# A two-layer decoder on one core: small matmuls of the mixer issued in whole groups, the last four gated heads kept in rows, keys' halves copied by DMA, and a reordered attention

## The chip, the core and the metric

The kernel runs on one core of a Trainium2 chip as a single program. The metric is device time in microseconds (us). The names of the engines in the profile are PE (TensorE, matmuls and transposes), PEld (its weight loads), DVE (VectorE), ACT (ScalarE), POOL (GpSimd) and SP (SyncE, whose queue issues nearly all DMAs).

## The reference

A decoder trunk for 512 tokens of width 1024. Layer 0 mixes tokens with a gated DeltaNet (8 query/key heads, 16 value heads of width 128), layer 1 with sliding-window attention over keys and values projected once (16 query heads, 4 key/value heads of width 64, window 128). Each layer ends with a gated MLP (inner width 2816) with a causal convolution.

```
def gated_deltanet(hn, w_in, conv_w, a_log, dt_bias, out_norm_w, w_out):
    proj = hn @ w_in
    qkv, z, b, a = split(proj)
    qkv = silu(causal_dwconv(qkv, conv_w))
    ...                                   # q, k, v; l2norm of q and k; beta, g
    o = chunked_gated_delta_rule(q, k, v, g, beta)
    o = rmsnorm(o, out_norm_w) * silu(z)
    return o @ w_out

def chunked_gated_delta_rule(q, k, v, g, beta):
    ...                                   # decay, m
    t_mat = triangular_solve(m + eye, eye)
    ...
    def step(state, inp):
        w_i, u_i, qd_i, kd_i, a_i, gl_i = inp
        v_new = u_i - w_i @ state
        o_i = qd_i @ state + a_i @ v_new
        state = state * gl_i + kd_i.T @ v_new
        return state, o_i

def sliding_window_sink_attention(hn, k, v, w_q, sinks, w_o, bias, mask):
    q = (hn @ w_q) * 64 ** -0.5
    s = where(mask, q @ band(k).T + bias, -1e30)
    m = maximum(max(s), sink)
    p = exp(s - m)
    o = (p / (sum(p) + exp(sink - m))) @ band(v)
    return o @ w_o
```

All of it is in float32.

## The kernel before

Activations lie transposed, 128 channels by 512 tokens to a tile. A large product is split in high and low parts: `cast` makes `whi` on ScalarE (line 132) and `wlo` on VectorE (133) from a loaded weight tile `stage`, and `mm3` issues three 128x512 matmuls for each slice of the contraction, hi·hi, hi·lo and lo·hi (lines 162 to 164, and 1181 to 1185 in attention, where they are yielded one by one). These are called dense products here. PSUM has eight banks under four names: `d` (three, dense products), `g` (two, transposes and small products), `s` (two), `p` (one).

**Mixer.** The 16 value heads go in four groups of four. The table `ORDER` is a list of jobs for each group: projections, key and query products, the triangular solve in 32x32 and then 64x64 tiles (`levels`, lines 570 to 597), four chunks of the scan (`scan`, 617 to 662), projections of the gates (z) and gates (g). A job's place in the table and `SHIFT` set the priority of its instructions; a scheduler then lays out each engine's queue by priority and by what is ready in its own cost model. So a job's instructions can be taken apart, and dense products of the next projection stand between them. `ORDER` and `SHIFT` are the same in both kernels.

In a chunk of the scan, TensorE makes `kS` and `qS` from the state `S` (line 617), `pu` from the solved tile (632), and after ScalarE has copied `pu` into `us` (636), `pS`, the product for the new state (640), and `po`, the output (657). The output goes to the scratch `od` in memory.

A gate (`gate`, 693 to 705) loads a head's output from `od` and its gate from `zd`, ScalarE scales the four quarters one by one (700), TensorE transposes each into bank `g` (703), VectorE multiplies (704), and the result is stored to `yd`. Heads 12 to 15 are gated last, behind the scan of the fourth group; they use the rows `dt` (four) and `va` (two). Then the output product `a_w_out` loads every head from `yd` (801) into rows `u`, splits it in hi and lo, loads and transposes x (821, copied at 822 by ScalarE) and adds the product to it.

**Attention.** Keys and values are projected (`attention`, 1140 on). The keys of each of the four heads are needed on both halves of the 128 partitions, since two query heads are multiplied at a time; ScalarE and VectorE write hi and lo of each half into both halves (1163 to 1167), with 64 partitions an instruction. Values are transposed at line 1171. From then on TensorE's order is written out by hand: for each of 16 steps `scores(u)` (1224), softmax on VectorE and ScalarE (1232 to 1253), `values(u - 2)` (1276), `turn_back(u - 1)`, which transposes the probabilities (1260), and 11 or 12 dense products of the next query projection or the first output tiles, by `take(stream, n)`. At the end come `values(14)`, `turn_back(15)`, `late_outputs` (1311), which ends three output tiles that were opened early, with `values(15)` before its last slice.

Between and behind these the MLPs are dense products nearly alone.

Of the kernel before, what the change touches and what calls it, by code (L numbers as in the profile page):

```python
# [41 lines left out]
def kernel(  # L42
# [137 lines left out]

    xs = []
# [25 lines left out]
    def columns(parts, n, s, q=SP, tag="acc"):  # L207
# [6 lines left out]
        ps = bank("g")  # L214
# [191 lines left out]
    def key_norms(g):  # L406
        pr = slice(2 * g, 2 * g + 2)
        st[g]["kk"] = pair("m32")
        for i in range(2):
            kT = st[g]["k"][:, i, :]  # L410
            ps = bank("g")
            for c in range(NC):
                cs = slice(c * P, (c + 1) * P)
                PE.matmul(ps[:, cs], kT[:, cs], kT[:, cs], start=True, stop=True)
# [59 lines left out]
    def query_norms(g):  # L474
        for i in range(2):
            ps = bank("g")
            junk = row("va")
            for c in range(NC):
                cs = slice(c * P, (c + 1) * P)
                PE.transpose(ps[:, cs], st[g]["q"][:, i, cs], ident[:])  # L480
                S.activation(junk[:, cs], ps[:, cs], AF.Square, accum_out=sse[:, 1, 2 * g + i, c : c + 1])
# [3 lines left out]
    def query_products(g, i):  # L485
        pq = bank("g")
        for c in range(NC):
            cs = slice(c * P, (c + 1) * P)
            PE.matmul(pq[:, cs], st[g]["k"][:, i, cs], st[g]["q"][:, i, cs], start=True, stop=True)
# [5 lines left out]
    def key_tokens(g, i):  # L495
        ps = bank("g")
        for c in range(NC):
            cs = slice(c * P, (c + 1) * P)
            PE.transpose(ps[:, cs], st[g]["k"][:, i, cs], ident[:])
# [10 lines left out]
    def value_proj(g, hh):  # L510
# [6 lines left out]
        for c in range(NC):  # L517
            cs = slice(c * P, (c + 1) * P)
            PE.transpose(ps[:, cs], v[:, cs], ident[:])
# [87 lines left out]
    def scan(g, c):  # L607
# [3 lines left out]
        hj = [(h, slice(h * P, (h + 1) * P)) for h in range(4)]  # L611
        if c > 0:
            kS, qS = bank("s"), bank("s")
            for x, t in ((kS, w["k"]), (qS, w["q"])):
                for i in range(2):
                    si = slice(256 * i, 256 * i + 256)
                    PE.matmul(x[:, si], t[:, i, cs], S0[:, si], start=True, stop=True)  # L617
            rr, qe = row("rq"), row("rq")
            for h, js in hj:
                V.scalar_tensor_tensor(  # L620
# [6 lines left out]
                )  # L627
            for h, js in hj:
                S.activation(qe[:, js], qS[:, js], AF.Copy, scale=egc[:, 4 * g + h, c : c + 1])
        pu = bank("s")  # L630
        for h, js in hj:
            PE.matmul(
                pu[:, js], w["y", h][:, cs], rr[:, js] if c > 0 else w["v", h][:, cs], start=True, stop=True
            )
        us = row("us")
        S.copy(us[:], pu[:])
        if c < NC - 1:
            pS = bank("p")
            for h, js in hj:
                PE.matmul(pS[:, js], w["kt", h][:, cs], us[:, js], start=True, stop=True)  # L640
            sn = row("S")
            if c == 0:
                V.tensor_copy(sn[:], pS[:])
            else:
                for h, js in hj:
                    V.scalar_tensor_tensor(
# [8 lines left out]
        po = bank("s")  # L655
        for h, js in hj:
# [752 lines left out]
```

## Time and profile before

| | |
|---|---|
| median of 3 runs | 1426.94 us (1426.77 to 1426.95) |
| profiled execution, its own time | 1428.72 us |
| span of the profiled execution | 1426.9 us |
| granted TensorE clock, mean | 0.998 |
| busy: PE, DVE, ACT | 1389.5, 1113.8, 753.8 us |
| mixer's heads, up to the end of the last scan | about 44 to 434 us |
| last gates, x, start of the output product | about 434 to 468 us |
| keys, values, attention | about 890 to 1028 us |

The span is from the first to the last instruction. In rows of a timeline stand the start, the length, the engine, the line, the operation with output<-inputs, the number of instructions that follow one another alike, and in brackets the idle time ahead and what ended it. A matmul in float32 has two records, so four products read x8; a transpose has one. Matmuls are pipelined: a row's length reaches from a matmul's start to its modelled end, and the next one starts earlier.

### The profile page before, as it was taken

The page shows a single profiled execution, that of the slowest core. Times are in us where ns is not written, and L with a number is a line of the kernel's source. Part 1 is how long each engine was busy: PE and PEld are TensorE (multiplying, and loading weights), DVE is VectorE, ACT ScalarE, POOL GpSimd, SP SyncE. Part 2 cuts the span into 40 slices and gives each one's busy share as a digit, 9 for nine tenths or more (in the row PEclk, how much of TensorE's full clock was granted, in tenths as well). Part 3 has the DMA queues.
Part 4 walks back from the last instruction along what each step waited for, and adds up shares of the span by engine and source line. Part 5 has one row for each costly group of instructions (what it writes and reads, how often), then busy time and mean ns, then how long its engine had stood idle before and what let it go on. Part 6 is the DMA issues. An engine that isn't in the chain of part 4 may idle for free.

```text
span 1426.9 us, 21762 instructions
## 1 busy us (share of the span) xinstructions
PE 1389.5 (97%) x8362; PEld 1165.5 (82%) x8362; DVE 1113.8 (78%) x2078; ACT 753.8 (53%) x1475; POOL 13.0 (1%) x37
## 2 busy tenths in 40 slices
PE   7999999999998999999999999999999999999997
PEld 5777878878876888888988889778788888988897
DVE  4996887969854447889878889878568888878996
ACT  7764566666546434444334446667544544344443
POOL 1000000000000000000000000000000000000000
PEclk9999999999999999999999999999999999999999
DMA  5324254264466324221443223122132322332222
GB/s 159 103 63 142 79 175 122 73 187 127 141 204 213 118 64 140 90 89 45 133 148 117 75 77 110 55 93 75 38 122 78 111 81 68 125 112 88 96 75 74
DMA packets 163131, 152.85 MB, mean 107 GB/s; under 512 B 24212, under 2 KB 150741, under 8 KB 163029
## 3 DMA queue, kind: packets, MB, share of 16 engines
q1 hardware_dynamic: 160770, 151.27, 33.0%
q8 instruction: 66, 1.08, 0.3%
q10 hardware_dynamic: 2259, 0.20, 0.1%
q14 instruction: 36, 0.29, 0.1%
HBM read 134.65 MB, written 16.80 MB: 106 GB/s over the span
## 4 chain that ended last, share of the span: by engine, by line
PE 82%; DVE 8%; DMA 6%; ACT 2%; issue 1%; DVEq 0%; SPq 0%; ACTq 0%
PE d L162 19%; PE d L163 19%; PE d L164 19%; DVE wlo L133 2%; PE s L617 1%; PE d L1030 1%; PE d L1185 1%; PE d L1028 1%; PE d L1183 1%; PE d L1181 1%; PE d L1029 1%; PE g L1260 1%; PE s L1030 1%; PE p L1276 1%; PE s L657 1%
## 5 line engine op out<-in xcount | busy, mean ns | idle before, releaser
L162 PE MATMUL d<-xh,whi 128*128 128x512 f32 x1128 | 445.1, 396 | 0.2
L163 PE MATMUL d<-xl,whi 128*128 128x512 f32 x1128 | 444.0, 395 | 0.0
L164 PE MATMUL d<-xh,wlo 128*128 128x512 f32 x1128 | 443.2, 395 | 0.7 <-DVE wlo L133 0.4
L132 ACT CAST whi<-stage 128x1024 fp32r<-128x1024 f32 (+2 forms) x234 | 227.3, 975 | 229.2 <-PE d L163 146.8
L133 DVE TENSOR_TENSOR wlo<-stage,whi 128x1024 fp32r<-128x1024 f32 (+2 forms) x234 | 263.5, 1129 | 66.7 <-ACT whi L132 66.2
L164 PEld LDWEIGHTS d<-xh,wlo 128*128 128x128 f32 x1128 | 211.6, 188 | 45.6 <-DVE wlo L133 1.1
L162 PEld LDWEIGHTS d<-xh,whi 128*128 128x128 f32 x1128 | 211.7, 188 | 44.1 <-ACT xh L172 0.5
L163 PEld LDWEIGHTS d<-xl,whi 128*128 128x128 f32 x1128 | 211.7, 188 | 42.9 <-issue 0.5
L260 DVE SCALAR_TENSOR_TENSOR acc<-d,cwc,acc 128x511 f32<-128x511 f32 (+2 forms) x96 | 70.7, 738 | 12.2 <-ACT acc L257 11.6
L911 ACT ACTIVATE dt<-dt 128x512 f32<-128x512 f32 x44 | 27.8, 632 | 80.1 <-DVE dt L894 80.1
L889 DVE TENSOR_TENSOR sz<-d,p6s 128x512 f32<-128x512 f32 x58 | 40.0, 689 | 36.9 <-PE d L164 35.0
L894 DVE SCALAR_TENSOR_TENSOR va<-sz,fcw,va 128x511 f32<-128x511 f32 (+1 forms) x58 | 43.4, 748 | 1.7 <-ACT va L892 0.9
L894 DVE SCALAR_TENSOR_TENSOR dt<-sz,fcw,dt 128x511 f32<-128x511 f32 (+1 forms) x58 | 43.4, 748 | 0.9
L546 DVE TENSOR_TENSOR sT<-sT,p6s 64x31 f32<-64x31 f32 (+15 forms) x124 | 40.8, 329 | 2.2 <-DVE p6s L540 0.3
L540 DVE TENSOR_TENSOR p6s<-sN,sT 64x31 f32<-64x31 f32 (+15 forms) x124 | 40.5, 327 | 2.4 <-DMA sN<-nd 0.4
L1249 ACT ACTIVATE dt<-dt,sm 128x256 f32<-128x256 f32 (+1 forms) x64 | 30.1, 471 | 19.2 <-DVE sm L1232 19.1
L132 ACT CAST whi<-st 128x768 fp32r<-128x768 f32 (+1 forms) x30 | 23.7, 792 | 30.1 <-PE p L1029 5.8
L889 DVE TENSOR_TENSOR zl<-d,p6s 128x512 f32<-128x512 f32 x30 | 20.7, 689 | 24.0 <-PE d L164 23.7
L665 ACT ACTIVATE rq<-o 128x128 f32<-128x128 f32 x64 | 19.0, 298 | 28.6 <-DVE o L660 16.0
L913 DVE TENSOR_TENSOR va<-dt,va 128x512 f32<-128x512 f32 x44 | 30.4, 691 | 1.2
L133 DVE TENSOR_TENSOR wlo<-st,whi 128x768 fp32r<-128x768 f32 (+1 forms) x30 | 26.9, 903 | 2.2 <-ACT whi L132 2.2
L892 ACT ACTIVATE dt<-sz,normc,fcw 128x512 f32<-128x512 f32 x29 | 23.6, 814 | 7.2 <-DVE sz L889 7.2
(770 smaller groups left out, 2866.7 us busy)
## 6 DMA issues: line engine op xcount, KB each, us to landing
stage<-in_ffn_w_up_dram SPq DMA_DIRECT2D x44, 1024.0 KB, 4.9
stage<-in_a_w_in_dram SPq DMA_DIRECT2D x23, 1024.0 KB, 5.1
stage<-in_ffn_w_down_dram SPq DMA_DIRECT2D x16, 768.0 KB, 6.1
stage<-in_a_w_out_dram SPq DMA_DIRECT2D x8, 1024.0 KB, 4.9
st<-in_ffn_w_down_dram SPq DMA_DIRECT2D x8, 768.0 KB
zd<-sz SPq DMA_DIRECT2D x16, 256.0 KB, 2.0
od<-o SPq DMA_DIRECT2D x16, 256.0 KB, 3.7
stage<-in_b_w_q_dram SPq DMA_DIRECT2D x4, 1024.0 KB
```

The lines of the kernel that those rows point to most:

```text
L132: S.copy(hi[:, :kt, :m], src)
L133: V.tensor_tensor(lo[:, :kt, :m], src, hi[:, :kt, :m].bitcast(F32), op=ALU.subtract)
L162: PE.matmul(ps, hi[:, k, :m], xh[k], start=first and k == 0, stop=False)
L163: PE.matmul(ps, hi[:, k, :m], xl[k][:], start=False, stop=False)
L164: done.append(PE.matmul(ps, lo[:, k, :m], xh[k], start=False, stop=last and k == kt - 1))
L260: V.scalar_tensor_tensor(acc[:, d:], ps[:, : T - d], col, acc[:, d:], op0=ALU.mult, op1=ALU.add)
L540: V.tensor_tensor(tv, N[:, s, s + 1 : 32].unsqueeze(2).to_broadcast([64, n, m]), Tm[:, s : s + 1, 0:m].to_broadcast([64, n, m]), op=ALU.mult,)
L546: V.tensor_tensor(Tm[:, s + 1 : 32, 0:m], Tm[:, s + 1 : 32, 0:m], tv, op=ALU.subtract)
L889: V.tensor_tensor(u[:], ps[:], rs[:], op=ALU.mult)
L894: V.scalar_tensor_tensor(acc[:, d:], u[:, : T - d], tap(2 - d, t), acc[:, d:], op0=ALU.mult, op1=ALU.add)
L913: V.tensor_tensor(b[:], a[:], b[:], op=ALU.mult)
L1249: S.activation(ej, ej, AF.Exp, bias=ngm[:, i : i + 1], scale=-1.0, accum_out=den[:, i : i + 1])
```

## The change

It has five parts.

1. A function `together` issues a group of small matmuls: the first with the order of issue behind the instructions given (the last that makes an input), the others behind the first, with a priority raised by `JUMP`, so that the scheduler lays the group out whole. `turn_row` does that for the four transposes of a row. They are used in key and query products, transposes of the mixer, the gates, the transposes of x, and the scan. The function `levels` is not edited.
2. In the scan `qS` is in bank `p`, `kS` and `qS` are one group behind the last piece of the state, `pu` is a group behind the last piece of `rr`, and `pS` and `po` are one group of eight.
3. The four last heads are gated in the rows `va`, `va`, `us` and `p6s`, and stay there for the output product; they are no longer stored to `yd` and loaded again.
4. A key pair's hi and lo are split once over 128 partitions, and four DMAs write the swapped halves. An Exp of one column goes ahead of the attention, and the values' transposes stand behind the fourth issue of `one_by_one`.
5. In the hand-written order, eight dense products go ahead of the first `turn_back` and four behind; at the end the outputs are split in other portions, and the last slice goes over the three tiles by kind of product instead of tile by tile.

```diff
+    def together(makes, *after):
+        first = None
+        for make in makes:
+            if first is None:
+                first = make()
+                for a in after:
+                    behind(first, a)
+            else:
+                with tc.high_priority(JUMP):
+                    behind(make(), first)
+
+    JUMP = 4000000
+
+    def turn_row(ps, src, *after):
+        cut = [slice(c * P, (c + 1) * P) for c in range(NC)]
+        together([lambda cs=cs: PE.transpose(ps[:, cs], src[:, cs], ident[:]) for cs in cut], *after)
...
     def scan(g, c):
-            kS, qS = bank("s"), bank("s")
+            kS, qS = bank("s"), bank("p")
+            terms = []
             for x, t in ((kS, w["k"]), (qS, w["q"])):
                 for i in range(2):
                     si = slice(256 * i, 256 * i + 256)
-                    PE.matmul(x[:, si], t[:, i, cs], S0[:, si], start=True, stop=True)
+                    terms.append((x[:, si], t[:, i, cs], S0[:, si]))
+            together([lambda a=a: PE.matmul(*a, start=True, stop=True) for a in terms], w["last"])
...
+        together([lambda a=a: PE.matmul(*a, start=True, stop=True) for a in terms], *last)
         us = row("us")
         S.copy(us[:], pu[:])
...
+            terms += [(pS[:, js], w["kt", h][:, cs], us[:, js]) for h, js in hj]
+        terms += [(po[:, js], w["at", h][:, cs], us[:, js]) for h, js in hj]
+        together([lambda a=a: PE.matmul(*a, start=True, stop=True) for a in terms])
...
     def gate(h):
-        ot, y = (row("ol"), row("zl")) if h < 12 else (row("dt"), row("va"))
+        ot = row("ol" if h < 12 else "dt")
+        y = row("zl") if h < 12 else row(("va", "va", "us", "p6s")[h - 12])
...
-            S.activation(ot[:, cs], ot[:, cs], AF.Copy, scale=f_c[:, h, c : c + 1])
+            scaled = S.activation(ot[:, cs], ot[:, cs], AF.Copy, scale=f_c[:, h, c : c + 1])
         pt = bank("g")
-        for c in range(NC):
-            PE.transpose(pt[:, c * P : (c + 1) * P], ot[:, c * P : (c + 1) * P], ident[:])
+        turn_row(pt, ot, scaled)
         V.scalar_tensor_tensor(y[:], pt[:], onw_c[:, 8:9], y[:], op0=ALU.mult, op1=ALU.mult)
-        SP.dma_start(yd[h], y[:])
+        if h < 12:
+            SP.dma_start(yd[h], y[:])
+        else:
+            gated[h] = y
...
-            yr = r2("u")
-            SP.dma_start(yr[:], yd[2 * h2 + j])
+            if h2 < 6:
+                yr = r2("u")
+                SP.dma_start(yr[:], yd[2 * h2 + j])
+            else:
+                yr = gated[2 * h2 + j]
             split(yr[:], a[:, j, :], b[:, j, :])
...
-                        S.copy(hi, src)
-                        S.copy(keys[g][far, 0, :], src)
-                        V.tensor_tensor(keys[g][near, 1, :], src, hi.bitcast(F32), op=ALU.subtract)
-                        V.tensor_tensor(keys[g][far, 1, :], src, hi.bitcast(F32), op=ALU.subtract)
+                    near, far = keys[i]
+                    split(f[:], near[:, 0, :], near[:, 1, :])
+                    for a, b in ((slice(0, 64), slice(64, 128)), (slice(64, 128), slice(0, 64))):
+                        SP.dma_start(far[a, :, :].bitcast(F32), near[b, :, :].bitcast(F32))
...
+        S.activation(warm[:], rs[:, 0:1], AF.Exp, scale=0.0)
...
+        for t in turned_values:
+            behind(t, issued[3])
...
                 if u > 1:
                     values(u - 2)
+                if u == 1:
+                    take(stream, 8)
                 if u > 0:
                     turn_back(u - 1)
-                take(stream, 12 if u < 12 else 11)
-            values(14)
+                take(stream, 4 if u == 1 else 12 if u < 12 else 11)
             for _ in stream:
                 pass
+            rest = late_outputs(opened, range(begun, KD - 1))
+            take(rest, 9)
             turn_back(15)
-            for k in range(begun, KD - 1):
-                for _ in late_outputs(opened, k):
-                    pass
+            values(14)
+            take(rest, 5)
             values(15)
-            for _ in late_outputs(opened, KD - 1):
+            for _ in rest:
                 pass
+            for i in range(3):
+                for m, (ps, w) in enumerate(opened):
+                    PE.matmul(ps[:], w[i % 2][:, KD - 1, :], (ah, ah, al)[i][-1], start=False, stop=i == 2)
+                    if i == 2:
+                        V.tensor_tensor(hT[m], hT[m], ps[:], op=ALU.add)
```

Three places of TensorE's queue show the change in order. First the solve of the fourth group, just ahead of its scan: `d` is the bank of a projection, `p` and `s` hold 64x64 tiles of the solve, `g` the transposes of a gate of an earlier group. Before:

```order
L164 MATMUL d_4405<-xh_142,wlo_4407 128x512
L703 MATMUL g_4126<-ident_81,ol_4118 128x128
L590 MATMUL p_4050<-Xg,nt_3418 64x64 x2
L703 MATMUL g_4126<-ident_81,ol_4118 128x128
L590 MATMUL p_4050<-Xg,nt_3418 64x64 x4
L703 MATMUL g_4126<-ident_81,ol_4118 128x128
L590 MATMUL p_4050<-Xg,nt_3418 64x64 x2
L703 MATMUL g_4126<-ident_81,ol_4118 128x128
L162 MATMUL d_4405<-xh_151,whi_4406 128x512
```

and the same products now, which have the lines 605 and 612:

```order
L164 MATMUL d_4404<-xh_160,wlo_4406 128x512
L605 MATMUL p_4050<-Xg,nt_3418 64x64 x8
L162 MATMUL d_4404<-xh_169,whi_4405 128x512
L163 MATMUL d_4404<-xl_170,whi_4405 128x512
L164 MATMUL d_4404<-xh_169,wlo_4406 128x512
L612 MATMUL s_4061<-sy_4001,p6s_347 64x64 x8
```

The eight small products stood in three pieces with transposes between, and are now one piece between dense products.

Second, the gates of heads 12 to 15 on TensorE, behind the last scan; `dt` is a scaled head, `d` the output product over the heads gated earlier. Before:

```order
L164 MATMUL d_4637<-sy_4522,wlo_4667 128x512
L703 MATMUL g_4332<-ident_81,dt_4324 128x128
L162 MATMUL d_4695<-kT_4512,whi_4696 128x512
L703 MATMUL g_4332<-ident_81,dt_4324 128x128 x2
L163 MATMUL d_4695<-qT_4513,whi_4696 128x512
L703 MATMUL g_4332<-ident_81,dt_4324 128x128
L164 MATMUL d_4695<-kT_4512,wlo_4697 128x512
L703 MATMUL g_4445<-ident_81,dt_4437 128x128
```

and now:

```order
L163 MATMUL d_4683<-qT_4509,whi_4684 128x512
L198 MATMUL g_4332<-ident_81,dt_4324 128x128 x4
L163 MATMUL d_4625<-at_4529,whi_4654 128x512
L164 MATMUL d_4625<-at_4528,wlo_4655 128x512
L164 MATMUL d_4683<-kT_4508,wlo_4685 128x512
L198 MATMUL g_4444<-ident_81,dt_4436 128x128 x4
```

The four transposes of a head are a whole group, with three dense products to the next head's, where they alternated with single dense products.

Third, the first `turn_back` in attention; `s` holds scores, `g` the transposed probabilities of step 0, `d` a query projection. Before:

```order
L1224 MATMUL s_8787<-kT_8384,S_8691 128x256
L1224 MATMUL s_8788<-kT_8384,S_8691 128x256
L1260 MATMUL g_8820<-ident_81,dt_8736 128x128 x2
L1260 MATMUL g_8825<-ident_81,dt_8743 128x128 x4
L1181 MATMUL d_8770<-xh_8639,whi_8771 128x512
```

and now, with eight dense products of which the first and the last two are shown in their place:

```order
L1251 MATMUL s_8768<-kT_8372,S_8672 128x256
L1251 MATMUL s_8769<-qT_8373,S_8672 128x256
L1207 MATMUL d_8751<-xh_8619,whi_8752 128x512
...
L1207 MATMUL d_8751<-xh_8627,whi_8752 128x512
L1209 MATMUL d_8751<-xl_8628,whi_8752 128x512
L1287 MATMUL g_8809<-ident_81,dt_8717 128x128 x2
L1287 MATMUL g_8814<-ident_81,dt_8724 128x128 x4
```

The transposes, which need the softmax of step 0, came right behind the scores of step 1, and now come behind eight dense products as well.

More of the change, by code (lines that the diff above doesn't have):

```diff
@@ L654, in scan @@
             w["S"] = sn
-        po = bank("s")
-        for h, js in hj:
-            PE.matmul(po[:, js], w["at", h][:, cs], us[:, js], start=True, stop=True)
         ot = row("o")
@@ L819 @@
         pt = bank("g")
-        for c in range(NC):
-            PE.transpose(pt[:, c * P : (c + 1) * P], x3[:, c, :], ident[:])
+        turn_row(pt, xrows[m])
         S.copy(hT[m], pt[:])
@@ L1141, in attention @@
         toep = rb[:]
[L1143 removed]
+        keys = [[wide("G") for u in range(2)] for i in range(2)]
         kxh, kxl = normed(h, NKV)
+        turned_values = []
         for kv in range(2):
```

70 lines of the change are left out of this document (31 added, 39 removed).

## The prediction

> **What bounds the kernel now.** I read the page first, then busy time by stretches, then TensorE's waits and the timeline around each. The page's first part says that TensorE is the bound:
>
> ```profile
> PE 1389.5 (97%) x8362; PEld 1165.5 (82%) x8362; DVE 1113.8 (78%) x2078; ACT 753.8 (53%) x1475; POOL 13.0 (1%) x37
> ```
>
> So only TensorE's own work and the 37 us in which it idles can be saved. The stretches that the change touches are the mixer up to its last chunks, the mixer's tail with the gated heads, the start of attention and its end. The columns are the window, its length, then busy time and count of each engine, granted clock, DMA.
>
> ```profile
> 44.00:420.00 376.00, 373.02 (x2685) 302.69 (x2686) 301.91 (x651) 231.93 (x594) 7.03 (x20) 1.00 0.42 128
> 420.00:470.00 50.00, 44.25 (x223) 34.23 (x222) 25.47 (x49) 30.51 (x82) 0.00 (x0) 0.97 0.62 200
> 900.00:945.00 45.00, 41.87 (x220) 32.11 (x219) 35.77 (x78) 30.41 (x62) 0.00 (x0) 1.00 0.25 81
> 1010.00:1035.00 25.00, 23.34 (x144) 17.76 (x143) 13.66 (x32) 12.20 (x26) 0.00 (x0) 1.00 0.19 62
> ```
>
> TensorE idles 3.0 us in the 376 of the mixer, where most of the grouping is done, but 5.8 in the tail, 3.1 at the start of attention and 1.7 at its end. The waits that carry this (us in total, times, longest):
>
> ```profile
> PE g L821 <- DVE va L704: 3.5, 1, 3.5
> ...
> PE g L1260 <- DVE dt L1253: 2.2, 1, 2.2
> ...
> PE g L703 <- ACT ol L700: 0.7, 2, 0.4
> ```
>
> A row of idle time understates a loss by some 0.16 us, since a dense matmul's row lasts 0.40 and the next starts after 0.24 (169.13 to 169.37 in the next lines).
>
> **Grouping 128-wide products.** Columns: start, us, engine, line, what, count. First a group of four transposes between dense products, then transposes that alternate with dense ones:
>
> ```profile
> 168.45 0.60 PE L499 MATMUL g<-ident,kT 128*128 128x128 f32 x4
> 168.81 0.49 PE L164 MATMUL d<-xh,wlo 128*128 128x512 f32 x1
> 169.13 0.40 PE L162 MATMUL d<-xh,whi 128*128 128x512 f32 x1
> 169.37 0.40 PE L163 MATMUL d<-xl,whi 128*128 128x512 f32 x1
> ```
>
> ```profile
> 444.28 0.27 PE L703 MATMUL g<-ident,dt 128*128 128x128 f32 x1
> ...
> 444.62 0.27 PE L703 MATMUL g<-ident,dt 128*128 128x128 f32 x1
> ```
>
> The group takes 169.13 - 168.45 - 0.24 = 0.44 us, 0.11 each. Singly, one dense and one transpose take 444.62 - 444.28 = 0.34, again about 0.1. So a split group costs nothing by itself, and holding these groups whole gains 0. What the hold can do is move waits: they come at the group's first member.
>
> **The solve's small tiles** are not grouped by the change, but transposes no longer stand between them. They do pay for each break:
>
> ```profile
> 399.51 0.40 PE L164 MATMUL d<-xh,wlo 128*128 128x512 f32 x1
> 399.83 0.68 PE L590 MATMUL p<-Xg,nt 64*64 64x64 f32 x16
> ...
> 400.78 0.39 PE L163 MATMUL d<-xl,whi 128*128 128x512 f32 x1
> ...
> 405.75 0.40 PE L164 MATMUL d<-xh,wlo 128*128 128x512 f32 x1
> ...
> 408.02 0.40 PE L163 MATMUL d<-xl,whi 128*128 128x512 f32 x1
> ```
>
> Whole, L590's 16 records and two dense products take 1.27 us. The same 16 in three pieces, with four transposes among them, take 2.27; less 4 x 0.11 that is 1.83, so 0.28 for each extra piece. Counted in the order, runs of small tiles go from 9, 9, 10, 14 in the four groups of heads to 9, 9, 9, 8. Seven fewer by 0.28 is **-2.0 us** (between 0, if each comes to stand alone in a wait anyway, and -3).
>
> **The tail.** First the last scan product and the first late gate, then ScalarE's scalings and one of the eight copies of x, then DMAs, then one window:
>
> ```profile
> 433.75 1.16 PE L657 MATMUL s<-us,at 128*128 128x128 f32 x8 [0.34 <-ACT us L636]
> ...
> 442.94 0.33 PE L703 MATMUL g<-ident,dt 128*128 128x128 f32 x1 [0.49 <-ACT dt L700]
> ```
>
> ```profile
> 442.49 4.79 ACT L700 ACTIVATE dt<-dt,fc 128x128 f32<-128x128 f32 x16 [0.57 <-DMA dt<-od]
> ...
> 460.12 0.59 ACT L822 COPY h<-g 128x512 f32<-128x512 f32 x1 [0.50 <-PE g L821]
> ```
>
> ```profile
> 438.76 3.65 DMA dt<-od
> ...
> 445.02 8.38 DMA yd<-va
> 453.42 2.53 DMA va<-zd
> ```
>
> ```profile
> 458.00:468.00 10.00, 9.91 (x50) 7.58 (x50) 2.83 (x5) 5.85 (x11) 0.00 (x0) 0.85 0.47 156
> ```
>
> Heads 14 and 15 wait for the two rows `va`, which are free only when heads 12 and 13 have been stored to `yd` (8.38 us); then 2.53 more bring `zd`. The transposes of x stand behind them in bank g, and the wait of L821 on L704 above is theirs: 3.5 + 0.16 = 3.7 us lost. Behind it the granted clock is 0.85 for 10 us: 1.5 us of clock lost. With the 0.49 + 0.16 at the first gate that makes 5.9. The Trainium skill ("TensorE: Matmul & The Clock Gate", section "Why this matters for your kernels") warns of TensorE gaps above some 3 us, after which the clock falls to half. This trace agrees that a gap of 3.5 is followed by a lower clock, though by 0.85 in the mean over 10 us. By that rule the 1.5 goes with the gap, as I count it; were a gap above 3 us left, the tail would gain 1.5 less.
>
> Now each of the four heads has a row of its own, so `zd` is loaded long before, and four stores and four loads of `yd` leave SP's queue. Two of the early loads, into `us` and `p6s`, wait there until these rows are free; the one into `us` stands ahead of the last `od` store, but waits for the products that this store's data need too, so I cost it at 0. What is late next is `dt<-od` and ScalarE: the 16 scalings take 4.79, 1.2 a head, and the first head's group now waits for all four of its quarters, until 442.49 + 1.2 = 443.7. TensorE was through with its dense products 0.49 + 0.16 before 442.94, at 442.3; counted in the order, 34 of them now stand between the last product of the scan (the eight of 433.75) and the first gate, for 32 before, so it comes at 442.8 and loses 0.9 + 0.16 = 1.1 us. The later heads come 1.2 apart with three dense products and a group, 3 x 0.24 + 0.44 = 1.2, between them. Then eight copies of x and four casts of the same size, 12 x 0.59 = 7.1 us of ScalarE, stand against TensorE's 11 dense products and 32 transposes, 6.2: 0.9 more. So 5.9 - 2.0 = **-3.9 us**; the ends are -5.9 and -2.0, if a wait of some 3 us stays.
>
> **Scans and gates of the other heads.** Each scan loses and gains waits: in the last one the products of `S` now have dense ones ahead, but one chunk's pu is followed at once by pS and po, which need `us`, copied by ScalarE (a copy as large as that at 460.12, 0.59). I take 0, between -2.7 (nearly all of the mixer's 3.0 of idling) and +4.
>
> **Attention's start.** Before, the keys' halves were cut and copied by 8 + 8 instructions of half height:
>
> ```profile
> 910.90 0.68 DVE L1166 TENSOR_TENSOR kT<-va,kT 64x512 fp32r<-64x512 f32 x1
> ...
> 923.04 1.23 DVE L133 TENSOR_TENSOR wlo<-stage,whi 128x1024 fp32r<-128x1024 f32 x1
> ```
>
> ```profile
> 917.28 1.25 PE L1171 MATMUL g<-ident,va 128*128 128x128 f32 x8 [0.63 <-DVE va L1158]
> ```
>
> Two of full height on each engine replace them: VectorE loses six of 0.70, 4.2 us, and the values that L1171 waits for are ready earlier; these transposes also move nine dense products back. Its wait and the slow starts around it go: **-1.2 us** (0 to -1.3). The four key DMAs of 256 KB are new. The nearest row is `dt<-od`, 256 KB in 3.65 us; from VectorE's split at about 912 they have until 929 to land, so 0. Behind them in SP's queue is the third load of query weights, which cannot start before 923.04 + 1.23 in the trace (its buffer) and so loses nothing. The early Exp on ScalarE moves a table load into time freed by six casts: 0.
>
> Then the softmax pipeline fills:
>
> ```profile
> 929.55 0.44 PE L1224 MATMUL s<-kT,rq 64*128 64x128 f32 x4
> ...
> 942.46 1.09 PE L1260 MATMUL g<-ident,dt 128*128 128x128 f32 x8
> ```
>
> ```profile
> 932.34 0.35 DVE L1232 CUSTOM_DVE_ANT_0 dt<-s,sz,nsink 128x128 f32<-128x128 f32 x1
> ...
> 1007.06 0.35 DVE L1232 CUSTOM_DVE_ANT_0 dt<-s,sz,nsink 128x128 f32<-128x128 f32 x1 [0.32 <-PE s L1224]
> ...
> 1009.86 1.01 DVE L1253 TENSOR_SCALAR dt<-dt,sm 128x128 f32<-128x128 f32 x4
> 1012.32 0.48 DVE L1232 CUSTOM_DVE_ANT_0 dt<-s,sz,nsink 128x256 f32<-128x256 f32 x1 [1.45 <-PE s L1224]
> ...
> 1015.46 1.14 DVE L1253 TENSOR_SCALAR dt<-dt,sm 128x256 f32<-128x256 f32 x4
> ```
>
> From the first scores to the second turn-back TensorE takes 12.9 us, of which some 2.8 are waits (3.1 of idling in the stretch, less the 0.63 above, and 0.16 behind each of two) and 10.1 work. The same work is done in the new order, but eight of the twelve dense products stand ahead of the first turn-back. What ends it then is two softmaxes in a row: 2.8 until VectorE starts (932.34 - 929.55), 3.8 for an even one (1007.06 to 1010.87), 4.3 for an odd one, 10.9. So **-2.0 us** (0 to -2.8).
>
> **Attention's end.**
>
> ```profile
> 1017.35 0.44 PE L1276 MATMUL p<-acc,Vp 128*64 128x128 f32 x4 [0.70 <-DVE at L169]
> ...
> 1025.36 0.50 PE L1181 MATMUL d<-at,whi 128*128 128x512 f32 x1 [0.69 <-ACT at L168]
> ```
>
> ```profile
> 1026.62 2.94 ACT L132 CAST whi<-stage 128x1024 fp32r<-128x1024 f32 x3 [1.31 <-PE d L1183]
> ```
>
> The move of the values behind the turn-back, and four dense products behind the last values, cover both waits and a smaller one: -2.2. But all three opened weight tiles are now read until the last three products, so the next casts (0.98 each) and VectorE's low part start some six products later: I estimate +1.4 by laying those rows behind the seventh of the nine. **-0.8 us** (-2.2 to +1.9).
>
> **Sum.** -2.0 - 3.9 + 0 - 1.2 - 2.0 - 0.8 = -9.9. The profiled execution took 1428.7 with a span of 1426.9, so it would take 1418.8; the median of the runs, 1426.94, lies 1.8 below it, so the runs would show 1417.0.
>
> **Rivals.**
> (1) The grouped mixer gives part back: whole groups leave fewer dense products in a scan's waits. For: the chunk where pS follows pu at once. Against: 3.0 us of idling in 376. Price +5 (the upper end above, and a wait as long as that at 433.75 in three more scans), so 1422.0.
> (2) The change doesn't do what it says in the tail and the fill: ScalarE's copies and `od` take `zd`'s place and VectorE's chain sets the fill as before. Then the tail keeps its wait of some 3 us (1.9 of the gain missing) and the fill's 2.0 are gone: 1420.9. For: ScalarE is busy 30.5 of 50 us there.
> (3) Slower: holding a gate's group until the fourth quarter is scaled costs up to three quarters of 0.30 us, 0.9, at each of 16 gates, 14.4 us. It outdoes the gain from 0.62 a gate on; in full, 1431.4. Against: only 0.7 us in two waits at L703 for the first twelve, and the order puts more dense products ahead.
>
> **How the numbers follow.** The forecast has 0.60, rivals 1 and 2 0.17 each, rival 3 0.06. A measurement here can tell about 0.2%, 2.9 us. The forecast's own bounds of scans, tail and end reach some 6 us below and 4 above; with rivals 1 and 2 the range is 1410.5 to 1423.5. Faster by over 0.2% (below 1424.1): the forecast and most of rivals 1 and 2, 0.88. Within 0.2%: what is left of these, 0.07. Slower: rival 3 past its point, 0.05.
>
> **What would show it.** Right: L704's successor waits for no DMA and the clock is 1.00 from 420 to 470; a single wait of 1 to 1.5 us at the first late gate; 35 runs of small tiles; under 1.2 us of waiting between the first scores and the second turn-back; a wait for whi of some 1 us after the last values. Wrong: TensorE's idling in 44 to 420 above 6 us, a gap over 3 us anywhere in the tail, or first scores that wait for a key DMA.

## The result, and the profile after

The changed kernel took 1416.98 us, median of 4 runs (1416.23 to 1418.66), beside 1426.95 for the kernel before on the same chip: a ratio of 0.9925, 95% interval 0.9909 to 0.994. The profiled execution took 1418.66 with a span of 1416.8, for 1428.72 and 1426.9 before, so 10.1 us are to be found in the two traces.

The page's busy times of the changed kernel:

```profile
PE 1384.8 (98%) x8362; PEld 1166.5 (82%) x8362; DVE 1109.1 (78%) x2072; ACT 748.0 (53%) x1470; POOL 15.7 (1%) x37
```

TensorE has the same 8362 records and is now idle for 32.0 us, not 37.4. So only 5.3 of the 10.1 us are idle time that the trace shows. Of the rest, 1.7 is the half clock that the tail no longer has, and some 3 are records of the mixer that start sooner after one another. The four stretches shown of before, the last two moved with the stage:

```profile
44.00:420.00 376.00, 371.15 (x2690) 303.91 (x2689) 304.91 (x656) 232.14 (x596) 9.66 (x20) 1.00 0.42 130
420.00:470.00 50.00, 47.70 (x247) 38.45 (x247) 28.10 (x51) 32.33 (x83) 0.00 (x0) 1.00 0.54 173
893.00:938.00 45.00, 44.85 (x253) 35.44 (x253) 33.52 (x77) 28.87 (x62) 0.00 (x0) 1.00 0.38 117
1002.00:1027.00 25.00, 23.88 (x147) 18.33 (x146) 14.41 (x30) 13.11 (x27) 0.00 (x0) 1.00 0.25 85
```

The tail went from 223 to 247 matmul records in 50 us and its clock from 0.97 to 1.00; the start of attention idles 0.15 us for 3.1. The mixer idles more than before, 4.9 us for 3.0. What TensorE waits for between 280 and 470 us, and at the end of attention:

```profile
PE d L162 <- ACT kT L168: 2.0, 1, 2.0
PE g L198 <- ACT ol L720: 1.5, 1, 1.5
PE p L659 <- ACT us L653: 1.5, 1, 1.5
PE g L198 <- ACT dt L720: 0.3, 1, 0.3
```

```profile
PE d L162 <- ACT whi L132: 1.1, 3, 0.7
```

L162 on kT waits for a load of `yd`, L198 on `ol` for a gate's load of `od`, L659 for `us` in the chunk where `pS` follows `pu` at once. The waits for rows `va` and for the softmax are gone.

Stage by stage, from the start of one row to the start of another in the two traces, with the nominal time of products that the change moved over a stage's border taken out:

| stage | before to after, us |
|---|---|
| start of the program, up to the last transpose of the input | +0.7 |
| mixer, up to the last scan product | -1.1 |
| tail and output product, up to the MLP's norm | -5.8 |
| up to the first scores (values, queries) | -1.2 |
| first scores to second turn-back | -2.4 |
| from there to the end | -0.1 |

They add up to -9.9. The start is not touched by the change: in the fourteen profiles here its last transpose begins between 16.1 and 18.0 us, whatever the kernel. The tail's borders are the last scan product and the matmul of the norm, here of the changed kernel, then of the one before (its scan product is the row at 433.75 above):

```profile
434.17 1.16 PE L659 MATMUL s<-us,at 128*128 128x128 f32 x8
...
528.79 0.69 PE L869 MATMUL g<-ones,ol 128*128 128x1 f32 x5
```

```profile
535.08 0.69 PE L845 MATMUL g<-ones,ol 128*128 128x1 f32 x5
```

That is 94.6 us for 101.3, of which 0.9 is dense work that now stands ahead of the scan product.

### The profile page after: what moved, and what is told of

It is laid out like the page before. It is cut to its first block, busy times and chain, and to the rows that moved or that the text cites. A ratio compares the mean times of both kernels' runs of the same rounds, so it can differ in the third digit from the quotient of the medians.

```text
span 1416.8 us, 21740 instructions
## 1 busy us (share of the span) xinstructions
PE 1384.8 (98%) x8362; PEld 1166.5 (82%) x8362; DVE 1109.1 (78%) x2072; ACT 748.0 (53%) x1470; POOL 15.7 (1%) x37
## 4 chain that ended last, share of the span: by engine, by line
PE 85%; DVE 7%; DMA 4%; ACT 2%; issue 1%; SPq 0%; DVEq 0%; ACTq 0%
PE d L162 20%; PE d L164 20%; PE d L163 20%; PE g L198 2%; DVE wlo L133 2%; PE d L1207 1%; PE d L1211 1%; PE d L1209 1%; PE d L1054 1%; PE d L1052 1%; PE d L1053 1%; PE s L1054 1%; PE p L1303 1%; PE s L659 1%; PE s L1052 1%
## 5 line engine op out<-in xcount | busy, mean ns | idle before, releaser
L162 PE MATMUL d<-xh,whi 128*128 128x512 f32 x1128 | 444.2, 394 | 0.2
L162 PEld LDWEIGHTS d<-xh,whi 128*128 128x128 f32 x1128 | 211.7, 188 | 44.8 <-ACT xh L172 0.5
```

Source lines behind the costliest of these rows:

```text
L162: PE.matmul(ps, hi[:, k, :m], xh[k], start=first and k == 0, stop=False)
```

## The experiments

All times are against the kernel before on the same chip in the same rounds; a ratio's interval is 95%, and 0.001 is 1.4 us. Most parts are worth 1 to 4 us, beside a scatter of single executions that is as large (31 of the kernel before, in the rounds of the first four runs, lay between 1424.1 and 1431.3). So the ratios carry the totals, and the traces the stages, each from a single execution.

**The late gates' part alone.** Parts 1, 2, 4 and 5 of the change are left out:

```diff
+        y = row("zl") if h < 12 else row(("va", "va", "us", "p6s")[h - 12])
...
+            gated[h] = y
```

> The kernel before with nothing changed but the last four gated heads: rows va, va, us and p6s, kept there, no yd store and load for them. Nothing is held in groups, the scan and the attention are as before. Theory A (the tail is most of the gain, 5.8 of 10.0 us, and needs no grouping): 1421.2 us, the wait of L821 on L704 (3.5 us) gone, no granted clock below 0.95 between 420 and 470, a wait at the first late gate of 0.3 to 0.7. Rival B (the tail gains only because its transposes come in whole groups): 1425 to 1427, a wait of over 2 us stays.

Measured: 0.9976 (0.9968 to 0.9985), -3.4 us. The tail stage fell by 5.5 us, the wait of L821 is gone with no group held, and the window has a full clock:

```profile
420.00:470.00 50.00, 47.68 (x252) 37.87 (x251) 30.63 (x54) 34.22 (x87) 0.00 (x0) 1.00 0.56 179
```

So theory A's stage holds, and the total is less than 5.8. In the profile some 3.3 us were lost elsewhere, at places that this edit does not touch. From 45.35 us the granted clock was 0.50 for 3.41 us, behind a wait of 1.75 us; all fourteen profiles have that wait near 44 us, at 1.62 to 1.93. And behind the 2.2 us wait of the first turn-back it was 0.50 again. In the run with only the groups held (below) the same wait was followed by 1.00. First rows of this run, then of that one:

```profile
PE g L1289 <- DVE dt L1282: 2.2, 1, 2.2
...
929.40:932.81 3.41, 1.20 (x12) 0.86 (x8) 2.79 (x14) 3.03 (x13) 0.00 (x0) 1.00 0.00 0
932.81:936.23 3.42, 3.42 (x11) 2.65 (x10) 1.70 (x9) 1.18 (x4) 0.00 (x0) 0.50 0.31 81
```

```profile
PE g L1275 <- DVE dt L1268: 2.2, 1, 2.2
...
930.74:934.16 3.42, 1.77 (x10) 1.52 (x11) 2.51 (x13) 2.85 (x12) 0.00 (x0) 1.00 0.02 5
934.16:937.57 3.41, 3.41 (x31) 2.63 (x32) 2.58 (x8) 2.01 (x5) 0.00 (x0) 1.00 0.28 77
```

**Own rows, with the round trip kept.** As the last, but every head is stored to `yd` and loaded again:

```diff
+        y = row("zl") if h < 12 else row(("va", "va", "us", "p6s")[h - 12])
...
         SP.dma_start(yd[h], y[:])
```

> As the kernel before, and the last four gated heads have the rows va, va, us and p6s, but each is still stored to yd and loaded again. Theory A1 (the 3.5 us wait is for the rows that the stores of heads 12 and 13 hold; own rows are enough): the wait of L821 on L704 goes, the loads of yd then feed the last products late, a wait of under 2 us for a cast of sy, at or vt: 1421 to 1423. Rival A2 (the round trip itself, 8.4 us of yd<-va and a load behind it, is what ends last): the wait moves to the products of heads 12 to 15 at 3 us or more and the clock falls again: 1425 to 1427.

Measured: 0.9988 (0.9979 to 0.9997), -1.7 us; the tail stage fell by 2.4. The wait for `va` is gone, and two waits for heads that come back from memory have taken its place:

```profile
PE d L162 <- ACT kT L168: 1.6, 1, 1.6
PE d L162 <- ACT ktok L168: 1.3, 1, 1.3
```

The waits and the full clock in the tail are theory A1's, but the total, some 1425.2 us, lies where rival A2 had it. In these profiles own rows give 2.4 of the stage and leaving out the round trip the other 3.1. This split is not firm: in the run with the eight dense products (below), whose tail is as before, the stage was 2.0 shorter as well.

**The groups alone.** Parts 1 and 2, with rows, `yd` and attention as before:

```diff
+            together([lambda a=a: PE.matmul(*a, start=True, stop=True) for a in terms], w["last"])
...
+        turn_row(pt, ot, scaled)
```

> The kernel before with only the groups of small matmuls held whole, in the whole mixer, the gates and the transposes of x, and the scan's banks and order of pS and po; rows of the late gates, yd and the attention as before. Theory A (fewer pieces of the solve, -2 to -3, against three waits in the mixer of 1.5 to 2.0 us each): 1426.0, within 1.5 of before, with waits of 1 us or more at a gate, at a pS and behind a load of yd. Rival C (the groups themselves bring the gain of the mixer and the tail): 1423 or less.

Measured: 0.9981 (0.9971 to 0.9991), -2.7 us, more than theory A had and less than rival C. The mixer stage fell by 1.2 in the trace, as in the changed kernel, with two of the three waits that I expected (1.5 at a `pS`, 1.1 at a gate, but 0.5 behind a load of `yd`). But the tail fell by 3.5 too, and I had given that stage to the rows alone:

```profile
PE g L198 <- DVE va L720: 0.7, 1, 0.7
```

That whole groups did this is not shown. VectorE's product for the first late gate starts 0.14 us sooner than before (444.10 for 444.24). The one for the third gate, which waits until a row `va` has been stored and loaded again, starts 3.2 sooner. First before, then this run:

```profile
456.07 0.75 DVE L704 SCALAR_TENSOR_TENSOR va<-g,onwc,va 128x512 f32<-128x512 f32 x1 [5.55 <-DMA va<-zd]
```

```profile
452.84 0.75 DVE L720 SCALAR_TENSOR_TENSOR va<-g,onwc,va 128x512 f32<-128x512 f32 x1 [3.51 <-DMA va<-zd]
```

From the first to the third are 8.7 us here and 11.8 before, but also 11.0 to 12.8 in the three other runs with the mixer of before, and 11.1 in the run that holds the gates' groups without the scan's (below). So most of the 3.5 goes with a store and a load that took less time. Whether that was chance, or the other order of the queues, the runs do not tell. In any case 3.5 and 5.5 are not 9: both take away the same wait.

**The keys' part alone.** One split, four DMAs, the early Exp, the values' transposes moved:

```diff
+                    split(f[:], near[:, 0, :], near[:, 1, :])
...
+        S.activation(warm[:], rs[:, 0:1], AF.Exp, scale=0.0)
```

> The kernel before with only the keys' part: one split over 128 partitions and four DMAs, the early Exp, the values' transposes behind the fourth issue of one_by_one. Theory A: the wait of L1171 (0.6) and the slow rows around it go, -1.2, so 1425.8, and the wait of the first turn-back on softmax stays near 2.2. Rival D (the key DMAs are late or the freed VectorE shortens the softmax's fill as well): first scores wait for a DMA, 1427 or more; or the first turn-back's wait falls under 1 us and the time to 1423.5.

Measured: 0.9976 (0.9965 to 0.9986), -3.4 us. No score waits for a key's DMA. But the first turn-back's wait fell as well, which I had not put on this part; the second half of rival D:

```profile
PE g L1283 <- DVE dt L1276: 0.8, 1, 0.8
```

**The early Exp alone.** One instruction is added to the kernel before:

```diff
+        S.activation(warm[:], rs[:, 0:1], AF.Exp, scale=0.0)
```

> The kernel before with one instruction more: an Exp of one column on ScalarE ahead of the attention. With it VectorE's queue ends the first softmax whole before it begins the second, where the two alternate before. Theory E (that order, and the 1.28 us table load taken out of the fill, shorten the first turn-back's wait; the keys only gave the rest of what the run with the keys' part gained): the wait of L1260 on dt falls from 2.2 to about 0.8 us, first scores to second turn-back from 12.9 to 11.5, total -1.4 us against before. Rival (the early Exp costs nothing and gains nothing, as my prediction had it; the fill was shortened by VectorE's freed 4.2 us): the wait stays at 2.2 and the time is within 0.5 us of before.

Measured: 0.9986 (0.9977 to 0.9995), -2.0 us, and the wait fell to 0.8 with the keys as before. So it is this instruction, not VectorE's freed time. First scores and second turn-back stand at 929.95 and 941.39, 11.4 us for 12.9. VectorE's queue, which in the kernel before takes up the second softmax before the first is scaled, now has the scalings of the first (x4) ahead:

```profile
935.49 1.01 DVE L1274 TENSOR_SCALAR dt<-dt,sm 128x128 f32<-128x128 f32 x4
936.42 0.48 DVE L1253 CUSTOM_DVE_ANT_0 dt<-s,sz,nsink 128x256 f32<-128x256 f32 x1
```

In the kernel before:

```profile
934.74 0.48 DVE L1232 CUSTOM_DVE_ANT_0 dt<-s,sz,nsink 128x256 f32<-128x256 f32 x1 [0.76 <-PE s L1224]
...
936.57 1.01 DVE L1253 TENSOR_SCALAR dt<-dt,sm 128x128 f32<-128x128 f32 x4
```

From the first row of this softmax on VectorE to its scaling are 2.8 us (932.70 to 935.49) for 4.2 (932.34 to 936.57), which is the whole gain of the fill. The 1.28 us table load, which theory E named beside the order, has no part in it. In the kernel before, ScalarE's first exponential still waits for VectorE when the load is done:

```profile
932.73 0.40 ACT L1249 ACTIVATE dt<-dt,sm 128x128 f32<-128x128 f32 x1 [0.35 <-DVE sm L1232]
```

That the scheduler lays the queue out in another way for this one instruction can be read from the order; why it does so was not tested.

**Eight dense products ahead of the first turn-back, alone.**

```diff
+                if u == 1:
+                    take(stream, 8)
...
+                take(stream, 4 if u == 1 else 12 if u < 12 else 11)
```

> The kernel before with only eight of twelve dense products moved ahead of the first turn-back. Theory (what I predicted of this part alone): first scores to second turn-back from 12.9 to 10.9 us, -2.0. With theory E VectorE still alternates between two softmaxes, so the first turn-back waits little but the second late: 11.0 to 11.5 us, -1.4 to -1.9. Rival (the wait only moves to the second turn-back): 12.5 or more, 0 to -0.4.

Measured: 0.9978 (0.9969 to 0.9988), -3.1 us. The fill took 940.60 - 929.55 = 11.05 us, -1.9 in the trace, what theory E gave; the wait is down to 0.2 and did not move to the second turn-back:

```profile
936.97 1.09 PE L1280 MATMUL g<-ident,dt 128*128 128x128 f32 x6 [0.16 <-DVE dt L1273]
...
940.60 1.09 PE L1280 MATMUL g<-ident,dt 128*128 128x128 f32 x8
```

With the Exp (-1.5) it gives -2.4 in the changed kernel, less than the sum, since both shorten one wait. The total of -3.1 holds some scatter of the tail, which is as before here and 2.0 us shorter in the trace: its wait of L821 was 1.9 us in this run, 2.8 and 4.2 in the two runs before it, and 3.5 in the first profile.

```profile
PE g L841 <- DVE va L724: 1.9, 1, 1.9
```

**The changed kernel without holding.** The function issues its members plainly:

```diff
-                for a in after:
-                    behind(first, a)
-            else:
-                with tc.high_priority(JUMP):
-                    behind(make(), first)
+            else:
+                make()
```

> The changed kernel with the function together issuing its members plainly, without order of issue and raised priority; banks and written order of the scan, rows of the late gates and attention as changed. Counted in the order it has 34 runs of small tiles of the solve, the changed kernel 35 and the one before 42. Theory P (fewer pieces of the solve come from the scan's banks and written order; holding groups gives nothing of its own and only moves waits): within 1.5 us of the changed kernel. Rival H (holding the groups is what gains in the mixer and keeps the tail short): 2 us or more slower than the changed kernel.

Measured: 0.9999 (0.999 to 1.0008), all of the gain lost; on the same chip the changed kernel stood at 0.9903, some 14 us lower. Theory P falls, clearly. The count of pieces was right and no measure: 34 runs of small tiles, one fewer than in the changed kernel, and yet the last scan product came at 445.9 us, 11.8 later than in the changed kernel's first profile (1.8 of this are eight more dense products ahead of it). Window of the mixer from the first scan on, of this kernel, then of the changed one in the same rounds:

```profile
148.00:447.00 299.00, 289.78 (x2085) 239.57 (x2085) 228.63 (x504) 177.96 (x482) 5.33 (x16) 0.98 0.46 139
```

```profile
148.00:433.00 285.00, 281.28 (x2070) 231.77 (x2070) 227.55 (x502) 176.15 (x479) 6.87 (x16) 1.00 0.47 144
```

9.2 us of idling for 3.7, and 0.98 of the clock. The waits there are those of products and transposes that stand too early in TensorE's queue, ahead of the result that they need:

```profile
PE g L195 <- ACT va L278: 3.0, 2, 1.8
...
PE g L430 <- ACT kT L278: 1.9, 1, 1.9
```

The clock costs more than the added idling. It was at half for 3.41 us from 277.0 and for 10.24 from 417.0, and ahead of the window for 3.41 from 44.9, together 8.5 us lost:

```profile
417.00:427.00 10.00, 9.04 (x100) 7.38 (x101) 6.20 (x10) 3.94 (x8) 0.30 (x1) 0.50 0.49 160
```

This is not one unlucky execution: the mean granted clock is 0.991 to 0.995 in all eleven of this kernel, and 0.998 or 0.999 in the four of the changed kernel in these rounds.

**The changed kernel again**, in these rounds:

> The changed kernel again, on the same chip and in the same rounds as the three others, as their measure: 10 us, 0.7%, below before; in its profile no TensorE gap above 2.0 us behind the first 20 us and no stretch at half the granted clock.

Measured: 0.9903 (0.9889 to 0.9918), 1416.22 us, with no gap over 2.0 us behind the first 20 and no stretch at half the clock. The two intervals of the changed kernel meet at 0.991, 13 us; between chips and rounds the gain is not known better than 10 to 14.

**Which groups.** First the scan's alone, then all others alone:

```diff
+            together([lambda a=a: PE.matmul(*a, start=True, stop=True) for a in terms], w["last"])
...
+        together([lambda a=a: PE.matmul(*a, start=True, stop=True) for a in terms])
```

> The kernel before with only the scan's groups: its banks, kS and qS as one group, pu, and pS with po as one group, all held; key and query products, transposes and gates as before, rows, yd and attention as before. Theory S (the scan's holds are what lays the mixer out well, since the same scan without holds idled 9.2 us in the mixer): 1.5 to 2.5 us below before, with 37 runs of small tiles, and the late gates' wait of L821 stays above 2 us. Rival G (the scan's groups need the others beside them): within 1 us of before or slower.

```diff
+        turn_row(ps, st[g]["k"][:, i, :])
...
+        turn_row(pt, ot, scaled)
```

> The kernel before with only the other groups held: key and query products, the mixer's transposes, the gates and the transposes of x, and the scan as before. Theory S: the tail gains some 3 us (whole gates give heads 12 and 13 to their stores earlier, the wait of L821 falls from 3.5 to under 1), the mixer loses 1 to 2 (a gate that waits whole for od): 1 to 2 us below before. Rival G2 (groups outside of the scan give nothing): within 0.5 us of before with L821's wait above 2 us.

Measured: the scan's 0.9989 (0.9974 to 1.0005), -1.6 us and not clear of none, with 37 runs of small tiles, a wait of 2.2 us at L821's successor and the mixer stage 2.0 shorter in the trace. The others 1.0041 (1.0026 to 1.0055), 5.9 us slower: my theory had them faster, and neither it nor its rival allowed for this. The tail gained nothing (it has 2.8 of the first line's waits), and the mixer stage took 6.1 more, 3.4 of it as two stretches at half clock, from 44.9 and from 277.0:

```profile
PE g L198 <- DVE va L718: 3.4, 2, 2.8
PE g L198 <- ACT va L281: 3.0, 2, 1.8
PE p L655 <- ACT us L651: 2.3, 2, 1.6
```

Holding these groups without the scan's thus puts waits of 1.1 to 1.8 us in the mixer; which of them does it was not tested. With both (0.9981) the mixer has two waits over 1 us from 148 us on, of 1.5 and 1.1, and nothing of the loss is left: parts of a schedule do not add.

**The end of attention as before, in the changed kernel:**

```diff
+            values(14)
             for _ in stream:
                 pass
-            rest = late_outputs(opened, range(begun, KD - 1))
-            take(rest, 9)
             turn_back(15)
```

> The changed kernel with the end of attention as before: values(14) ahead of the last dense products, turn_back(15), eighteen dense products, values(15), the last slice tile by tile. My prediction had the new end at -0.8 (2.2 of waits covered, 1.4 of casts moved back): then 0.8 slower than the changed kernel. By the traces the new end has traded waits of 0.70, 0.69 and 0.22 for waits for whi of 0.68, 0.22 and 0.22, worth 0.2 to 0.6. Rival (the end matters as a whole 2 us): 2 slower.

Measured: 0.9931 (0.9914 to 0.9947), between 0 and 4 us slower than the changed kernel, whose two ratios differ by as much. From the second turn-back to the start of TensorE's last product the trace has 478.1 us, for 477.5 in both profiles of the changed kernel, so some 0.6 is what the new end is worth, by one profile.

**Another order of the last slice:**

```diff
-            for i in range(3):
-                for m, (ps, w) in enumerate(opened):
+            for m, i in ((0, 0), (0, 1), (1, 0), (0, 2), (1, 1), (2, 0), (1, 2), (2, 1), (2, 2)):
+                ps, w = opened[m]
```

> The changed kernel with the last slice in another order: hi and lo of tile 0 with the high part, hi of tile 1, then tile 0 with the low part, and so on, so that the first weight tile is free after four of nine products, not seven. If the three waits for whi (0.68, 0.22, 0.22) come from the late release of the tiles, they go and the kernel is 0.9 to 1.1 us faster than the changed one, at 0.9% below before. Rival (VectorE's low parts of the next tiles, not the release, set the pace): the waits turn into waits for wlo and nothing is gained.

Measured: 0.9916 (0.9901 to 0.993), not to be told from the changed kernel. The longest wait for whi is gone, two short ones stay, and none for wlo has come; the stretch is 0.5 us shorter, half of what I expected:

```profile
PE d L162 <- ACT whi L132: 0.4, 2, 0.2
```

## Why the prediction was right, and where it was not

The total, 1417.0, agrees with the measured 1416.98 more closely than its terms do. The tail and the fill gave 2.3 us more than the sum has, the mixer, the end and the start of the program 2.3 less. That these cancel is luck, and in the second rounds the gain was some 14 us and not 10. In the range, the upper bounds of scans, tail and end add to 8.6 us, not to 4.

- **Solve, -2.0, with scans and gates at 0: measured -1.1 together.** There are 35 runs of small tiles, as counted. In the changed kernel's trace sixteen records between dense products again lie in one piece:

```profile
399.96 0.39 PE L162 MATMUL d<-xh,whi 128*128 128x512 f32 x1
400.28 0.68 PE L605 MATMUL p<-Xg,nt 64*64 64x64 f32 x16
400.89 0.50 PE L163 MATMUL d<-xl,whi 128*128 128x512 f32 x1
```

What failed is the step "I take 0" for scans and gates: idling in the window rose by 1.9 us, part of what rival 1 priced, with 1.45 at the chunk that I named and 1.52 at a gate that I had not. A third wait, 1.98 for a load of `yd`, stands behind the window and ahead of the last scan product. The rest of the stage, in which no idling shows, is 3.0 us shorter, 3.2 in the second profile. So the fewer breaks are worth the 2.0 of the sum or more, if the other groups have no share in it. The four profiles of this mixer lie 2.8 us shorter to 2.1 longer than the one of before, so -1.1 is one draw of these. Three stretches at half clock, 1.7 us each, stand in the two longest of the four.

- **A split group costs nothing, so holding gains 0 by itself: wrong as a statement on the change.** The 0.11 a record stands, but holding decides the layout, and the same code without it is some 14 us slower, in its trace more by half clock (8.5 us) than by idling. I read the change as grouping instructions, and what mattered was where the scheduler put all the others. I had priced the clock in the tail alone.

- **The tail, -3.9: measured -5.8**, close to its lower end (-5.0 to -5.8 in the four profiles with this mixer and tail). The wait and the half clock went as said, and what is late next is the first gate, as said. Of the two costs I set against the gain, the gate's is right in size but not in form, and the single wait of 1 to 1.5 us that I named as a sign did not come. TensorE comes at 443.4, and the group starts with the first scaled quarter, not the fourth, and is then paced by ScalarE's 0.30 (0.96 from its start to the next dense product, where the second group took 0.39):

```profile
443.24 4.79 ACT L720 ACTIVATE dt<-dt,fc 128x128 f32<-128x128 f32 x16 [1.30 <-DMA dt<-od]
```

```profile
443.70 1.21 PE L198 MATMUL g<-ident,dt 128*128 128x128 f32 x4 [0.28 <-ACT dt L720]
444.66 0.48 PE L163 MATMUL d<-at,whi 128*128 128x512 f32 x1
...
445.44 0.64 PE L198 MATMUL g<-ident,dt 128*128 128x128 f32 x4
```

"Behind" is an order of issue and no wait. The 0.9 for copies of x did not come. The 0.9 a gate of rival 3 fell with the same reading, though groups without the scan's did end slower, by layout.

- **Attention's start, -1.2: measured -1.2.** No key's DMA was late. That the sizes agree to 0.1 is a draw: this stage, which holds an MLP as well, is 1.1 to 2.4 us shorter in the six profiles with this part, and 0.4 shorter to 1.2 longer in the seven other runs without it.

- **Fill, -2.0: measured -2.4.** The stage of before idles 2.2 us, not the 2.5 that I took from a longer window, so its work is 10.5 and not 10.1. The two softmaxes in a row (10.9) do not end it either: in the changed kernel TensorE idles 0.02 us from 922.11 to 932.64, so its own work does. And the early Exp, which I set at 0, is worth 1.5 of the wait alone; without it VectorE's order is not the one that the sum used, and the fill takes 11.05.

- **End, -0.8: measured -0.1 against before, 0.6 against the old end in the changed kernel.** The three waits for whi came as said, 1.1 us for the 1.4 that I took.

The start of the program, +0.7 in these two profiles, is scatter that no step had.

## What to carry to other kernels

Where a scheduler lays out the queues, an edit that only ties instructions together is priced by the queue that it gives: count the dense work between each producer and its consumer on the busiest engine, before and after, and not the instructions saved. Two edits that remove one wait do not add, and two edits that are bad or neutral singly can be good together, so test the parts both alone and left out. A gap on the engine that bounds the kernel can cost more than its length, when the clock falls behind it. A wait read from one profile is one draw: the same wait for `va` was 1.9, 2.8, 3.5 and 4.2 us in four profiles of the same mixer.

## What the runs showed of the hardware

TensorE's granted clock is 1.00 or 0.50 here. A half lasts 3.41 us, which costs up to 1.7, and can follow idle stretches far shorter than the 3.5 us of before. The run with the old end of attention had 1.6 us of idling at a gate and then 3.41 at half:

```profile
300.68 1.35 PE L198 MATMUL g<-ident,ol 128*128 128x128 f32 x4 [1.63 <-ACT ol L720]
```

```profile
298.13:301.55 3.42, 1.79 (x8) 0.84 (x6) 1.80 (x3) 1.32 (x5) 0.00 (x0) 1.00 0.58 186
301.55:304.96 3.41, 3.41 (x10) 2.73 (x10) 0.75 (x1) 0.48 (x1) 0.00 (x0) 0.50 1.07 376
```

In the changed kernel's first profile the same wait, 1.52, and another of 1.98 at 426 were followed by a full clock.

The traces show what decides. In each of the fourteen, all changes of the clock from the first full clock on (between 12.8 and 16.4 us) lie whole multiples of 3.41 us apart. I call such a period a window. Between the start and the last matmuls there are 18 halves, 17 of one window and one of three. Counted over all windows at full clock, the next one was at half behind all 12 that held 1.85 us or more of TensorE idling (by the modelled ends), behind 6 of the 23 that held 1.39 to 1.77, and behind none of the 3986 that held 1.32 or less. So it matters how much of a wait falls into one window. The 2.2 us at the first turn-back lie whole in one in the run with the late gates (2.21 idle up to 932.81), and are cut by a border in the run with the groups (1.65 idle up to 934.16); the rows of both stand in the first experiment. Where the borders fall differs from execution to execution: the wait near 44 us was followed by a half in six of the fourteen profiles. The same wait thus costs up to 1.7 us more in some executions and nothing more in others.

The Trainium skill ("TensorE: Matmul & The Clock Gate", section "What's actually happening") has a monitor with a free-running window of about 3.4 us, which would make the outcome depend on the phase. The traces agree with the half rate, with the window's length and with an outcome that depends on the phase. The idle window of 3.4 us that the page gives for going cold is not borne out: 1.85 of 3.41 us were always enough, and 1.39 once.
